# A two-layer streaming-encoder trunk on one core: the rows for the experts' gather are stored with even columns ahead of odd ones, by ScalarE copies, and the experts' transposes read neighbouring columns

## The chip, the cores and the metric

The kernel runs on one core of one Trainium2 chip. The metric is the device time of one execution, in microseconds; lower is better. TensorE (PE) multiplies and transposes, VectorE (DVE) and ScalarE (ACT) work elementwise, GpSimd (POOL) does small work and the gathers, SyncE (SP) issues the loads and stores. Each of these runs its own list of instructions in order; semaphores tie the lists together.

## The reference

Two layers, each on a residual stream `h` of 512 tokens by 1024 columns. Three kinds of attention mix the tokens; the first norm follows, then a router that picks two of 16 experts for every token, then the experts and a gated per-layer embedding, and the second norm.

```python
for i in range(DEPTH):                                  # DEPTH = 2
    ...                                                 # three mixers give mix
    h = layer_norm(DEEPNORM_ALPHA * h + mix, ln1_g[i], ln1_b[i])
    ffn = grouped_moe(h, router_w, router_b, w_gate[i], w_up[i], w_down[i])
    ple = jax.nn.sigmoid(h @ ple_gate[i]) * (p[i] @ ple_proj[i])
    h = layer_norm(DEEPNORM_ALPHA * h + ffn + ple, ln2_g[i], ln2_b[i])

def grouped_moe(h, router_w, router_b, w_gate, w_up, w_down):
    scores = jax.nn.sigmoid((h @ router_w).astype(jnp.float32))
    ...                                                 # best group of four, top 2 in it: gate
    for e in range(N_EXPERTS):                          # 16 experts
        hid = jax.nn.silu(h @ w_gate[e]) * (h @ w_up[e])
        out = out + gate[..., e:e + 1] * (hid @ w_down[e])
    return out
```

## The kernel before, in words

The 512 tokens lie in four tiles of 128 rows, the whole row of 1024 fp32 columns in each (`VB`, `base(t)`). All large products are made of three matmuls each (`mm3`, lines 213 to 215): every operand is split into a high part, cast by ACT, and a low part, the difference, made by VectorE. `split` (L193) does that for activations, `convert` (L201 and L203) for the weights, 1024 columns at a time out of raw buffers (`RAW`, `raw`) that SyncE's loads fill. A raw buffer is loaded again once the subtract of L203 has read it.

In each layer the last part ahead of the experts goes tile by tile, in the order that the string `MLA_REST` names: `n3 n2 n1 t3 l3 n0 t2 l2 t1 l1 t0 l0`.

- `n`: `first_norm(t)` projects the mixers' output, takes the norm (square on ACT at L942, `z` on VectorE at L944, a tile of the pool `w4`, four buffers) and writes the normed row back into `VB` (L951, two halves). Then SyncE stores the row in DRAM (L953, `h1_d`), from where the experts gather it.
- `t`: `rows_to_T` transposes the row in two groups of four (L229, PSUM tags `tr` and `av`) and splits both groups (L193).
- `l`: `logits` multiplies the transposed row by the router's weights (L957, L958).

Behind the last tile stand the router (ACT copies the logits out at L983 as `lgs`; VectorE makes scores, picks and ranks, L984 to L1043; one-hot masks `ohs` at L1050; PE turns them into the table `ti` of token numbers for every expert, L1053 and L1055; the gates end at L1083, and PE's L1060 reads them) and, on PE between all that, the products of the first quarter of the per-layer embedding (`embed`, "mm<-RA" and "s<-RA" 128x256, with ACT's tanh at L922 and VectorE's L923 and L929).

An expert has room for 112 tokens. `fetch_tokens` gathers its rows by an indirect DMA on GpSimd (L1094), which waits for all four stores and for `ti`. `turn_tokens` transposes them eight times (L1126). The gate and up weights are loaded with two neighbouring rows side by side, `"e (j p r) c -> e p j (r c)"` with r=2, so that the contraction index on partition p of piece (j, r) is 256 j + 2 p + r. The transposes therefore read every second column of the gathered row:

```python
def pair_columns(k):
    return slice(256 * (k // 2) + k % 2, 256 * (k // 2 + 1), 2)
```

Then 48 matmuls for gate and up and 24 for down follow, with the hidden rows transposed by four at L1252, and the rows are added into DRAM by an indirect DMA. Expert 0's weights are converted early: the first gate chunk and the up chunk (`raw`) stand among the last tiles' work on ACT and VectorE.

A list scheduler decides when the program is built in which order each engine's instructions stand, by its own estimates; a change of one piece can shift others on every engine. `after(x, [y])` in the code only asks it to keep x behind y.

Of the kernel before, what the change touches and what calls it, by code (L numbers as in the profile page):

```python
# [24 lines left out]
CAP = 112  # L25
# [61 lines left out]
def tile_kernel(ctx, tc, A, out):  # L87
    nc = tc.nc
    V, SC, PE, G = nc.vector, nc.scalar, nc.tensor, nc.gpsimd
# [35 lines left out]
    ID = CT[:, C_ID:C_ID + 128]  # L125
# [6 lines left out]
    h1_d = [dr.tile([S, D], F32, name=f"h1_{i}") for i in range(L)]  # L132
# [4 lines left out]
    def acc(tag="mm"):  # L137
        return ps.tile([128, 512], F32, tag=tag, name=tag)
# [4 lines left out]
    def after(later, earlier, wait=mybir.DependencyClass.NoSync):  # L143

        for e in earlier:
            tc.add_manual_dep(later.ins, e.ins.name, mybir.DependencyInfo(wait, mybir.DependencyReason.DATA),
                              reason="order")
# [19 lines left out]
    tsl = lambda t: slice(t * 128, (t + 1) * 128)  # L167
# [55 lines left out]
    def rows_to_T(row, t, tags=("tr", "tr"), behind=()):  # L223

        subs, his = [], []
        for g in range(2):
            p = acc(tags[g]).rearrange("p (j n) -> p j n", j=4)
            for j in range(4):
                after(PE.transpose(p[:, j], row[:, tsl(4 * g + j)], ID), behind)  # L229
            hi, lo = [R(HS[2 * i + g], 0, 2048, 4)[:, :, tsl(t)] for i in range(2)]  # L230
            done = split(p, hi, lo)
            subs.append(done[1])
            his.append(done[0])
        return subs, his

    def base(t, a=0, b=1024):
        return VB[:, t * 1024 + a:t * 1024 + b]
# [198 lines left out]
    for l in range(L):  # L436
# [407 lines left out]
        for c in ORDER:  # L844
# [10 lines left out]
            elif c == "E":  # L855
# [3 lines left out]
                for i in range(2):  # L859
                    half, t = todo.pop(0)  # L860
# [23 lines left out]
        for kd in range(2):  # L884
            p = trp()
# [48 lines left out]
        def first_norm(t):  # L934
            row = base(t)
            sums = sm.tile([128, 3], F32, name="sums")
            for half in range(2):
                project_o(WO[half], half, t, LATE, 1.0, sums[:, half:half + 1])
            nm = sm.tile([128, 1], F32, name="nm")
            V.tensor_scalar(nm, sums[:, 0:1], sums[:, 1:2], -1.0 / 1024, op0=OP.add, op1=OP.mult)  # L940
            sq = RAW[:, 2, :1024]
            squares[t] = SC.activation(sq, row, AF.Square, bias=nm, accum_out=sums[:, 2:3])  # L942
            z = w4.tile([128, 1024], F32, name="z", tag="w4")
            V.scalar_tensor_tensor(z, row, nm, LN[:, :1024], op0=OP.add, op1=OP.mult)  # L944
            ve = sm.tile([128, 1], F32, name="ve")
            V.tensor_scalar(ve, sums[:, 2:3], 1.0 / 1024, EPS, op0=OP.mult, op1=OP.add)
            rs = sm.tile([128, 1], F32, name="rs")
            pows[t] = G.tensor_tensor(rs, ve, HALF[:, 0:1], op=OP.pow)
            for i in range(2):
                c = slice(512 * i, 512 * i + 512)  # L950
                V.scalar_tensor_tensor(row[:, c], z[:, c], rs, LN[:, 1024 + c.start:1024 + c.stop],  # L951
                                       op0=OP.mult, op1=OP.add)
            nc.sync.dma_start(h1_d[l][tsl(t), :], row)  # L953

        def logits(t):
            for k in range(8):
                PE.matmul(plg[:, t, :32], hT(0, k)[:, tsl(t)], RW[:, k], start=k == 0, stop=False)  # L957
                PE.matmul(plg[:, t, :16], hT(1, k)[:, tsl(t)], RW[:, k, :16], start=False, stop=k == 7)  # L958

        plg = None  # L960
        for c in MLA_REST.split():
            t = int(c[1])
            if c[0] == "a":
                attend_mla(t)
            elif c[0] == "n":
                first_norm(t)
            elif c[0] == "t":
                subs, his = rows_to_T(base(t), t, tags=("tr", "av"))
            elif c[0] == "l":
                if plg is None:  # L970
                    plg = acc("av").rearrange("p (t e) -> p t e", t=4)
                logits(t)
# [133 lines left out]

        def pair_columns(k):
            return slice(256 * (k // 2) + k % 2, 256 * (k // 2 + 1), 2)  # L1110

        def fetch_tokens(e):
            if e == 0:
                xg = raw_chunk([], 1024)[:CAP]
# [6 lines left out]
        def turn_tokens(e, xg):  # L1121
            xh, xl = [R(8 + e % 2, o, 8 * CAP, 8) for o in (0, 1024)]
            for g in range(2):
                p = trp()
                for jj in range(4):
                    PE.transpose(p[:, jj, :CAP], xg[:, pair_columns(4 * g + jj)], ID[:CAP, :CAP])  # L1126
                split(p[:, :, :CAP], xh[:, 4 * g:4 * g + 4], xl[:, 4 * g:4 * g + 4])
            return xh, xl

# [31 lines left out]
        def overflow():  # L1161

            most = nc.values_load(cmi[0:1, 0:1], min_val=0, max_val=S)
            with tc.If(most > CAP, label=f"over{l}"):
                for j in range(1, 5):
                    to, _, *slots_ = slot_tables(j, "o")
                    go = slot_gates(*slots_, "o")
                    nc.sync.dma_start(ov_d[l][0, j - 1].rearrange("e s -> s e"), to)
                    nc.sync.dma_start(ov_d[l][1, j - 1].rearrange("e s -> s e"), go.bitcast(I32))
                i = state["ring"][0]  # L1170
                W = (RAW[:, i] if i < NRAW else state[f"raw{i}"]).rearrange("p (k c) -> p k c", k=4)
                W2 = W.rearrange("p k c -> p (k c)").rearrange("p (k c) -> p k c", k=2)
                with tc.For_i(0, NE, 1) as e:
                    for j in range(4):
                        idx = []
                        for i in range(2):
                            ix = sm.tile([128, 1], I32, name=f"ix{i}")
                            nc.sync.dma_start(ix, ov_d[l][i, j, bass.ds(e, 1), :].rearrange("e s -> s e"))
                            idx.append(ix)
                        xg = w4.tile([128, 1024], F32, name="xg", tag="w4")  # L1180
                        G.memset(xg, 0.0)
                        gather(xg, idx[0])
                        xt = w4.tile([128, 8, 128], F32, name="xt", tag="w4")
                        for g in range(2):
                            p = trp()
                            for jj in range(4):
                                PE.transpose(p[:, jj], xg[:, pair_columns(4 * g + jj)], ID)
                            SC.copy(xt[:, 4 * g:4 * g + 4], p)
                        pgu = []
                        for w in (wgt, wup):  # L1190
                            p = acc("s")
                            for i in range(2):
                                nc.sync.dma_start(
                                    W2, w[bass.ds(e, 1), :, 2 * i:2 * i + 2].rearrange("e p j c -> (e p) j c"))
                                for k in range(4):
                                    PE.matmul(p, xt[:, 4 * i + k], W[:, k], start=i + k == 0, stop=i + k == 4)
                            pgu.append(p)
                        sg = w2.tile([128, 512], F32, name="sg", tag="w2")
                        SC.activation(sg, pgu[0], AF.Silu)
                        V.tensor_tensor(sg, sg, pgu[1], op=OP.mult)  # L1200
                        p = trp()
                        for kd in range(4):
                            PE.transpose(p[:, kd], sg[:, tsl(kd)], ID)
                        ht = w2.tile([128, 4, 128], F32, name="ht", tag="w2")
                        SC.copy(ht, p)
                        yt = w4.tile([128, 1024], F32, name="yt", tag="w4")
                        py = [acc("s") for _ in range(2)]
                        for i in range(2):
                            nc.sync.dma_start(W2, wdn[bass.ds(e, 1), :, 2 * i:2 * i + 2].rearrange("e p k c -> (e p) k c"))
                            for half in range(2):  # L1210
                                for k in range(2):
                                    PE.matmul(py[half], ht[:, 2 * i + k], W2[:, k, half * 512:half * 512 + 512],
                                              start=i + k == 0, stop=i + k == 2)
                        for half in range(2):
                            V.tensor_scalar(yt[:, half * 512:half * 512 + 512], py[half], idx[1].bitcast(F32), None,
                                            op0=OP.mult)
                        scatter(yt, idx[0], y_d[l])
# [11 lines left out]
        xg = fetch_tokens(0)  # L1229
# [8 lines left out]
        for e in range(NE):  # L1238
# [38 lines left out]
            if e + 1 == NE:  # L1277
# [25 lines left out]
                for half in range(2):  # L1303
                    c = slice(512 * half, 512 * half + 512)
# [146 lines left out]
```

## Time and profile before

| | |
|---|---|
| time, median of 3 runs | 1342.89 us (1337.99 to 1343.95) |
| profiled execution | 1344.58 us, its span 1342.8 us, mean granted PE clock 0.976 |
| PE busy | 1284.1 us (96%), 6828 instructions |
| VectorE busy | 1002.9 us (75%) |
| ScalarE busy | 833.8 us (62%) |
| GpSimd busy | 229.3 us (17%) |
| layer 0: last tiles and router | about 262 to 326 us |
| layer 0: experts | about 326 to 665 us |
| layer 1: last tiles and router | about 930 to 985 us |
| layer 1: experts | about 985 to 1320 us |

The busy shares are averages over stages with different limits, so the windows by stage and the timelines of single stretches are read beside them. In a timeline, a row gives the start, the duration, the engine, the line, the operation with its tiles, and in brackets the idle time of the engine ahead of it with what ended it. Matmuls are pipelined, so the distance from one start to the next says more than a duration. Lines in rows are those of the kernel before; the change moves the later ones by 8 or 9 (L958 becomes L966, L983 L992, L1050 L1059, L1055 L1064) and those from `turn_tokens` on by 6 (L1126 becomes L1132).

### The profile page before, as it was taken

The numbers are of one execution on the slowest core, as the hardware profiler recorded it, in microseconds if no ns is written. First come the engines' busy times: TensorE is split into PE (matmuls) and PEld (weight loads), VectorE is DVE, ScalarE is ACT, GpSimd is POOL, SyncE is SP. The second block draws the span as 40 slices with busy tenths as digits, with TensorE's granted clock in tenths as the row PEclk, the third lists the DMA queues.
The fourth block names the chain that finished last, engine by engine and source line by source line (L and its number), as shares of the span: only waits on it lengthen the run. The fifth ranks groups of instructions, "written<-read, shape, count | busy, mean of one in ns | idle before, by whom it ended". The sixth has DMA issues, their size and how long they took to land. (4 is left out here: it accounts for less than half of the span.)

```text
span 1342.8 us, 19139 instructions
## 1 busy us (share of the span) xinstructions
PE 1284.1 (96%) x6828; PEld 1012.9 (75%) x6828; DVE 1002.9 (75%) x1754; ACT 833.8 (62%) x1348; POOL 229.3 (17%) x209
## 2 busy tenths in 40 slices
PE   7899999998999999999889999999989999999996
PEld 6677776777787887777777777767878878778774
DVE  5645768677879879987775557676779797888985
ACT  4544645443868768886444556354467685886873
POOL 2301210001212212222001021200012121221311
PEclk9999998998999999999989999889989999999999
DMA  7732533234989979999763222341469898997983
GB/s 210 263 96 57 194 107 110 94 115 174 331 300 357 368 269 365 368 339 315 269 203 79 64 75 80 87 150 51 164 225 366 289 359 313 337 365 287 381 300 133
DMA packets 126215, 302.36 MB, mean 225 GB/s; under 512 B 13245, under 2 KB 56013, under 8 KB 126112
## 3 DMA queue, kind: packets, MB, share of 16 engines
q1 hardware_dynamic: 115400, 278.29, 57.8%
q0 software_dynamic: 9840, 21.15, 6.5%
q10 hardware_dynamic: 872, 1.62, 0.4%
q8 instruction: 55, 0.90, 0.3%
q14 instruction: 48, 0.39, 0.1%
HBM read 284.92 MB, written 30.39 MB: 235 GB/s over the span
## 5 line engine op out<-in xcount | busy, mean ns | idle before, releaser
L201 ACT CAST RA<-RAW 128x1024 fp32r<-128x1024 f32 x252 | 257.3, 1050 | 67.2 <-PE mm L215 22.9
L203 DVE TENSOR_TENSOR RA<-RAW,RA 128x1024 fp32r<-128x1024 f32 x190 | 227.5, 1222 | 59.3 <-ACT RA L201 56.3
L201 ACT CAST RA<-raw 128x1024 fp32r<-128x1024 f32 x190 | 195.7, 1048 | 61.6 <-PE mm L215 31.5
L203 DVE TENSOR_TENSOR RA<-raw,RA 128x1024 fp32r<-128x1024 f32 x142 | 168.9, 1220 | 21.2 <-ACT RA L201 20.8
L213 PE MATMUL mm<-RA,slot 128*112 128x512 f32 (+2 forms) x424 | 175.6, 415 | 4.3 <-ACT RAW L740 3.2
L215 PE MATMUL mm<-RA 128*128 128x512 f32 (+1 forms) x400 | 153.5, 384 | 0.7 <-DVE RA L193 0.7
L215 PE MATMUL mm<-RA,slot 128*112 128x512 f32 (+2 forms) x360 | 146.5, 407 | 0.0
L1099 POOL DMA_INDIRECT y<-yt,ti x30 | 64.6, 2152 | 476.0 <-ACT yt L1275 476.0
L214 PE MATMUL mm<-RA,slot 128*112 128x512 f32 (+2 forms) x344 | 141.3, 411 | 0.9 <-DVE RA L203 0.9
L213 PE MATMUL mm<-RA 128*128 128x512 f32 (+1 forms) x336 | 127.8, 381 | 5.9 <-ACT RA L201 3.7
L214 PE MATMUL mm<-RA 128*128 128x512 f32 (+1 forms) x336 | 126.7, 377 | 2.1 <-DVE RA L203 2.1
L213 PE MATMUL av<-RA 128*112 128x512 f32 x256 | 103.4, 404 | 0.8 <-ACT RA L201 0.8
L215 PE MATMUL av<-RA 128*112 128x512 f32 x256 | 101.8, 397 | 0.7 <-DVE RA L193 0.6
L213 PEld LDWEIGHTS mm<-RA,slot 128*112 128x112 f32 (+1 forms) x424 | 79.6, 188 | 26.5 <-ACT RAW L740 4.2
L213 PE MATMUL s<-RA,ht 128*112 128x512 f32 x240 | 94.9, 395 | 0.4 <-ACT ht L193 0.4
L215 PE MATMUL s<-RA,ht 128*112 128x512 f32 x240 | 94.6, 394 | 0.0
L215 PEld LDWEIGHTS mm<-RA 128*128 128x128 f32 x400 | 77.5, 194 | 12.6 <-issue 2.4
L215 PEld LDWEIGHTS mm<-RA,slot 128*112 128x112 f32 (+1 forms) x360 | 66.7, 185 | 19.7 <-issue 0.9
L214 PEld LDWEIGHTS mm<-RA,slot 128*112 128x112 f32 (+1 forms) x344 | 65.3, 190 | 18.1 <-issue 1.7
L203 DVE TENSOR_TENSOR slot<-RAW,RA 128x1024 fp32r<-128x1024 f32 x62 | 73.7, 1220 | 6.5 <-ACT RA L201 6.5
L213 PEld LDWEIGHTS mm<-RA 128*128 128x128 f32 x336 | 65.4, 195 | 15.3 <-ACT RA L201 4.1
L213 PE MATMUL s<-RA 128*128 128x256 f32 (+3 forms) x256 | 75.6, 296 | 0.5 <-ACT RA L193 0.3
(425 smaller groups left out, 2888.6 us busy)
## 6 DMA issues: line engine op xcount, KB each, us to landing
RAW<-in_w_gate_dram SPq DMA_DIRECT2D x56, 1024.0 KB
raw<-in_w_down_dram SPq DMA_DIRECT2D x45, 1024.0 KB
raw<-in_w_up_dram SPq DMA_DIRECT2D x40, 1024.0 KB
RAW<-in_w_up_dram SPq DMA_DIRECT2D x24, 1024.0 KB
RAW<-in_w_down_dram SPq DMA_DIRECT2D x19, 1024.0 KB
RAW<-in_w_in_dram SPq DMA_DIRECT2D x26, 512.0 KB
RAW<-in_w_o_dram SPq DMA_DIRECT2D x16, 512.0 KB
raw<-in_w_gate_dram SPq DMA_DIRECT2D x8, 1024.0 KB
```

The lines of the kernel that those rows point to most:

```text
L201: cast = SC.copy(hi[:, a:b], raw[:, a:b])
L203: state["subs"] = [V.tensor_sub(lo[:, a:b], raw[:, a:b], f32(hi[:, a:b]))]
L213: PE.matmul(o, sh, mh, start=start, stop=False)
L214: PE.matmul(o, sh, ml, start=False, stop=False)
L215: return PE.matmul(o, sl, mh, start=False, stop=stop)
L1099: G.indirect_dma_start(out=dst, out_offset=bass.IndirectOffsetOnAxis(ap=idx.bitcast(U32), axis=0), in_=src, in_offset=None, bounds_check=S ...
```

## The change

The store of a normed row moves from `first_norm` to a new function `store_rows`, which runs behind `rows_to_T` of the same tile. It copies the row from `VB` into `z` with two ACT copies of 128x512; in every block of 256 columns the 128 even ones come first and the 128 odd ones behind. The copies are asked to stand behind both casts of the tile. SyncE then stores `z`. The transposes of the gathered rows take neighbouring columns (`tsl`), since what was column 256 j + 2 p + r is now column 256 j + 128 r + p. `VB` itself keeps its order. (The last edit is in the path for experts with over 112 tokens, which these inputs do not take.)

```diff
-            nc.sync.dma_start(h1_d[l][tsl(t), :], row)
+            return z
+
+        def store_rows(t, z, behind):
+
+            for i in range(2):
+                c = slice(512 * i, 512 * i + 512)
+                after(SC.copy(z[:, c].rearrange("p (j r i) -> p j r i", j=2, r=2),
+                              base(t)[:, c].rearrange("p (j i r) -> p j r i", j=2, r=2)), behind)
+            nc.sync.dma_start(h1_d[l][tsl(t), :], z)
...
-        plg = None
+        plg, normed = None, {}
...
-                first_norm(t)
+                normed[t] = first_norm(t)
             elif c[0] == "t":
                 subs, his = rows_to_T(base(t), t, tags=("tr", "av"))
+                store_rows(t, normed[t], his)
...
-        def pair_columns(k):
-            return slice(256 * (k // 2) + k % 2, 256 * (k // 2 + 1), 2)
-
...
-                    PE.transpose(p[:, jj, :CAP], xg[:, pair_columns(4 * g + jj)], ID[:CAP, :CAP])
+                    PE.transpose(p[:, jj, :CAP], xg[:, tsl(4 * g + jj)], ID[:CAP, :CAP])
...
-                                PE.transpose(p[:, jj], xg[:, pair_columns(4 * g + jj)], ID)
+                                PE.transpose(p[:, jj], xg[:, tsl(4 * g + jj)], ID)
```

With this the scheduler's order comes out differently in the stretch ahead of the experts. Below stands the order of the instructions, by line, operation and tiles, without times.

ScalarE, layer 0, from the cast of the projection weights to the logits' copy and what follows it, before. L193 casts are those of `split` (`tr` and `av` are the two halves of a tile's transposes, `pj` the embedding's projection weights), L201 casts those of weights, L911 scales a finished row:

```order
L193 CAST pj<-pr__4185 128x512
L201 CAST RA<-RAW 128x1024 x2
L193 CAST RA<-av 128x4x128
L193 CAST RA<-tr 128x4x128
L911 ACTIVATE VB<-VB 128x256 x2
L193 CAST RA<-av 128x4x128
L201 CAST RA<-RAW 128x1024 x2
L983 COPY lgs<-av 128x128
L911 ACTIVATE VB<-VB 128x256
L985 ACTIVATE sco<-sco 128x64
```

The same place in the changed kernel:

```order
L193 CAST pj<-pr__4193 128x512
L201 CAST RA<-RAW 128x1024
L193 CAST RA<-av 128x4x128
L959 COPY z<-VB 128x512 x2
L193 CAST RA<-tr 128x4x128
L201 CAST RA<-RAW 128x1024
L911 ACTIVATE VB<-VB 128x256 x2
L193 CAST RA<-av 128x4x128
L959 COPY z<-VB 128x512 x2
L201 CAST RA<-RAW 128x1024
L992 COPY lgs<-av 128x128
L201 CAST RA<-RAW 128x1024
```

The copies of tiles 1 and 0 (L959) stand in between (tile 2's stand just ahead, tile 3's further up), and one of the two weight casts that stood right ahead of `lgs` now stands behind it.

VectorE, layer 0, in the router's chain from the ranks' operand `B` to the token table `ti`, before:

```order
L1038 TENSOR_TENSOR B<-oh,CT 128x8x16
L1042 TENSOR_TENSOR tmp<-oh,av 128x128
L1089 TENSOR_REDUCE cmx<-av 128x1
L1043 TENSOR_REDUCE rank<-tmp 128x8
L1091 CAST cmi<-cmx 128x1
L1050 TENSOR_SCALAR ohs<-IOB,rank 128x128 x8
L1070 TENSOR_TENSOR tmp<-oh,sco 128x128
L923 SCALAR_TENSOR_TENSOR th<-th,s 128x256
L1055 TENSOR_SCALAR ti<-av 128x16
```

And before, further down on the same engine, behind the last of the gates (`B<-oh,gb`), the two subtracts of the raw up-weights (`RA<-raw`):

```order
L929 SCALAR_TENSOR_TENSOR VB<-VB,th 128x256
L1083 TENSOR_TENSOR B<-oh,gb 128x8x16
L203 TENSOR_TENSOR RA<-raw_4308,RA 128x1024
L1064 TENSOR_TENSOR gs<-vv 128x16
L203 TENSOR_TENSOR RA<-raw_4308,RA 128x1024
L1065 TENSOR_TENSOR gs<-gs,vv 128x16
```

The chain from `B` to `ti` in the changed kernel:

```order
L1047 TENSOR_TENSOR B<-oh,CT 128x8x16
L203 TENSOR_TENSOR RA<-raw_4316,RA 128x1024
L1051 TENSOR_TENSOR tmp<-oh,av 128x128
L1098 TENSOR_REDUCE cmx<-av 128x1
L1052 TENSOR_REDUCE rank<-tmp 128x8
L1100 CAST cmi<-cmx 128x1
L203 TENSOR_TENSOR RA<-raw_4316,RA 128x1024
L1059 TENSOR_SCALAR ohs<-IOB,rank 128x128 x8
L1079 TENSOR_TENSOR tmp<-oh,sco 128x128
L923 SCALAR_TENSOR_TENSOR th<-th,s 128x256
L1064 TENSOR_SCALAR ti<-av 128x16
```

Both subtracts of `raw` now stand inside the chain: one ahead of `tmp`, one ahead of the masks `ohs`. In layer 1 only one of them does, the one ahead of `ohs`.

On TensorE nine more of embed's 128x256 matmuls stand ahead of the second group of transposes of the last tile, so ahead of the last logits; the matmuls that turn `ohs` into `ti`, which alternated with embed's last ones, stand behind all of these; and those that make the ranks stand 11 places further back. On SyncE the load of expert 0's remaining up-weights, which waits for the second subtract, still follows the four stores and the loads it followed before.

## Rows read from the trace of the kernel before

**Rows 1.** The page: busy time by engine; GB/s in 40 slices of the span.

```profile
PE 1284.1 (96%) x6828; PEld 1012.9 (75%) x6828; DVE 1002.9 (75%) x1754; ACT 833.8 (62%) x1348; POOL 229.3 (17%) x209
...
GB/s 210 263 96 57 194 107 110 94 115 174 331 300 357 368 269 365 368 339 315 269 203 79 64 75 80 87 150 51 164 225 366 289 359 313 337 365 287 381 300 133
```

**Rows 2.** Windows: PE, PEld, DVE, ACT, POOL busy; PE clock; DMA share; GB/s.

```profile
302.00:326.00 24.00, 19.33 (x182) 18.68 (x180) 20.13 (x78) 9.37 (x18) 1.40 (x2) 0.94 0.37 130
...
500.00:600.00 100.00, 100.00 (x465) 76.74 (x464) 89.78 (x92) 84.61 (x101) 24.02 (x15) 1.00 0.98 354
```

**Rows 3.** Waits of PE, 326 to 665 us: total, times, longest (first row).

```profile
PE av L213 <- ACT RA L201: 0.8, 1, 0.8
```

**Rows 4.** Groups by line and shape, weight loads: busy, mean ns | idle before.

```profile
L1126 PEld LDWEIGHTS trp<-CT,xg 112*128 112x128 f32 x240 | 33.4, 211 | 2.9
...
L1252 PEld LDWEIGHTS trp<-CT,sg 112*128 112x128 f32 x128 | 15.0, 140 | 5.7 <-DVE sg L1243 1.2
```

**Rows 5.** Timeline of PE: two transpose groups and the matmul behind each.

```profile
334.07 1.09 PE L1126 MATMUL trp<-CT,xg 112*128 112x112 f32 x8
334.93 0.46 PE L215 MATMUL mm<-RA,slot 128*112 128x512 f32 x1
...
343.82 0.55 PE L1252 MATMUL trp<-CT,sg 112*128 112x112 f32 x4
344.14 0.46 PE L213 MATMUL av<-RA 128*112 128x512 f32 x1
```

**Rows 6.** Timeline of PE: the first expert's transposes, layer 0.

```profile
324.51 1.74 PE L1126 MATMUL trp<-CT,RAW 112*128 112x112 f32 x8 [1.38 <-DMA RAW<-h,ti]
...
326.12 0.77 PE L213 MATMUL mm<-RA,slot 128*112 128x512 f32 x1
```

**Rows 7.** Timeline of ACT: a cast that waits for its load.

```profile
637.71 2.00 ACT L201 CAST RA<-RAW 128x1024 fp32r<-128x1024 f32 x2 [1.74 <-DMA RAW<-in_w_up_dram]
```

**Rows 8.** Timeline of ACT: last tiles of layer 0 up to the logits' copy.

```profile
295.86 0.59 ACT L193 CAST RA<-tr 128x512 fp32r<-128x512 f32 x1 [5.97 <-PE tr L229]
...
298.43 0.64 ACT L193 CAST pj<-pr__4185 128x512 fp32r<-128x512 f32 x1
298.95 2.01 ACT L201 CAST RA<-RAW 128x1024 fp32r<-128x1024 f32 x2
...
305.13 0.59 ACT L193 CAST RA<-av 128x512 fp32r<-128x512 f32 x1 [2.31 <-PE av L229]
...
308.00 0.27 ACT L983 COPY lgs<-av 128x128 f32<-128x128 f32 x1 [0.39 <-PE av L958]
```

**Rows 9.** Timeline of PE: the first and the eleventh of a run of embed matmuls.

```profile
310.04 0.28 PE L214 MATMUL s<-RA 128*128 128x256 f32 x1
...
311.23 0.28 PE L215 MATMUL s<-RA 128*128 128x256 f32 x1
```

**Rows 10.** Timeline of DVE: the router's chain in layer 0, and behind it.

```profile
309.89 0.19 DVE L986 TENSOR_SCALAR sco<-sco 128x64 f32<-128x64 f32 x1
...
314.94 0.28 DVE L1038 TENSOR_TENSOR B<-oh,CT 128x128 bf16<-128x128 f32 x1
315.72 0.29 DVE L1042 TENSOR_TENSOR tmp<-oh,av 128x128 f32<-128x128 f32 x1 [0.50 <-PE av L1035]
...
316.37 1.40 DVE L1050 TENSOR_SCALAR ohs<-IOB,rank 128x128 bf16<-128x128 bf16 x8
...
318.82 0.17 DVE L1055 TENSOR_SCALAR ti<-av 128x16 int32<-128x16 f32 x1 [0.53 <-PE av L1053]
...
322.63 1.22 DVE L203 TENSOR_TENSOR RA<-raw,RA 128x1024 fp32r<-128x1024 f32 x1
```

**Rows 11.** Timeline of ACT: the two casts ahead of those subtracts.

```profile
316.18 1.05 ACT L201 CAST RA<-raw 128x1024 fp32r<-128x1024 f32 x1 [7.04 <-PE mm L215]
...
318.50 1.05 ACT L201 CAST RA<-raw 128x1024 fp32r<-128x1024 f32 x1 [0.44 <-PE mm L215]
```

**Rows 12.** Timeline of POOL: the first expert's gather, layer 0.

```profile
319.88 1.12 POOL L1094 DMA_INDIRECT RAW<-h,ti  x1 [20.90 <-DVE den L1075]
```

## The prediction

> **What bounds the kernel now.** I read the page's first section, then the windows by stage, then who waits for whom in the longest stage, and last the timelines of the two places that the diff touches. The page's first line shows TensorE busy for 1284.1 of 1342.8 us, VectorE for 1002.9 [rows 1]. The windows say where that share is not full: from 500 to 600 us, with the first layer's experts running, PE is busy for the whole 100 us, while between 302 and 326 us, where that layer's router runs, it has 19.33 of 24 us [rows 2]. So there are two kinds of place. In the expert stage every nanosecond taken from PE comes off the time: the largest wait of PE's in the first layer's is a single one of 0.8 us [rows 3]. In the router's stretch of each layer the time is a chain: last tile's logits, VectorE's scores and ranks, the token table, the gather, the first expert's transposes. A delay of that chain counts in full, because PE has nothing else left.
>
> **What the transposes give.** The 240 LDWEIGHTS of `turn_tokens` that read every second column of a gathered row take 211 ns, the 128 of L1252, of the same 112x128 shape from neighbouring columns, 140 ns [rows 4]. These lie beside matmuls, so I do not count their busy time but the distance between starts. A group of eight transposes starts at 334.07 and the matmul behind it at 334.93: 0.86 us. A group of four from neighbouring columns starts at 343.82 and the next matmul at 344.14: 0.32, so 0.64 for eight [rows 5]. That is 0.22 us for an expert, and 240/8 = 30 experts make 6.6 us. The first expert of each layer is left: its eight start at 324.51, and the next matmul at 326.12, 1.61 us for eight, on an engine that had just waited [rows 6]. Between nothing and the same quarter of 1.61 us (0.4) I take 0.2 for each, 0.4 together.
>
> Not all of it stays. Late in layer 0 the ACT casts of weights wait for their loads, 1.74 us at 637.71 [rows 7], and PE's wait of 0.8 us is one for such a cast [rows 3]. What the last four experts of that layer would give, 4 x 0.22 = 0.9 us, I take as lost to the loads. Bounds: nothing lost, or all 3.3 us of the layer. The transposes give 6.6 + 0.4 - 0.9 = **6.1 us** (bounds 3.7 and 7.0).
>
> **What the copies cost.** Sixteen ACT copies of 128x512 are new, eight for a layer. No row shows a copy with a stride of two. The nearest are the ACT cast of pj, 128x512, 0.64 us and 0.52 us to the next start, and twice that, 1.05 us, the time of a 128x1024 cast, for the other end [rows 8, 11]. I take 0.52, the row of the same shape; a tile's pair is then 1.05 us. In layer 0 the pair of tile 3 falls into an idle stretch of 5.97 us. The pairs of tiles 2 and 1 push the later casts by 2.1 us, and the idle time of 2.31 us ahead of the last cast takes these 2.1 in [rows 8]. The pair of tile 0 stands ahead of `lgs`, but of the two weight casts that stood between (such a pair takes 2.01 us) one has moved behind `lgs`. ACT is therefore ready at about 308.7, and is not what `lgs` waits for.
>
> What it waits for is PE, where nine more embed matmuls stand ahead of the last tile's second transposes. They run 0.12 us apart (ten from 310.04 to 311.23) [rows 9], so `lgs` moves from 308.00 to 309.05: **+1.05**. The cast that moved behind `lgs` and its subtract (1.05 + 1.22 us) then hold up L986, which stands behind that subtract on VectorE: about 311.5 instead of 309.89, +1.6 [rows 10].
>
> Now the largest term. Both subtracts of the raw chunk (expert 0's first up-weights), of which the first ran at 322.63, behind everything the router needs, 1.22 us each, stand in the middle of the router's chain in the changed order: one ahead of L1042, one ahead of the eight `ohs` of L1050 [rows 10]. Each waits for an ACT cast, and the casts wait for the embed matmuls that last read the same slots: 316.18 after 7.04 us of idleness, 318.50 after 0.44 [rows 11]. With `B` of L1038 at 316.55 (314.94 + 1.6) and the first cast done by 316.9, the first subtract ends at 317.9, and L1042 starts there, where it was at 315.72: +2.2. The second cast waits for the last embed matmul, which comes earlier than before, since the `ohs` matmuls no longer stand between: 317.65 to 318.7. Its subtract ends at 319.85, and `ohs` starts at 319.9 instead of 316.37: +3.5. From `ohs` to `ti` it took 2.45 us, 0.53 of it a wait for matmuls that alternated with embed's; alone on PE they follow the masks at once, so 1.85, and `ti` moves from 318.82 to 321.75, **+2.9** [rows 10]. The gather at 319.88 [rows 12] and the transposes at 324.51 [rows 6] follow it by the same 2.9.
>
> Layer 1 repeats the pattern, but only one subtract stands in the chain there: the same steps give +2.3. The front costs 2.9 + 2.3 = **5.2 us**. Lower bound: `lgs` late by 1.05 and the subtracts' 2.44 or 1.22, less the 0.50 + 0.53 us that the chain waits now [rows 10], so 2.5 + 1.2 = 3.7. A gain is excluded, because work is added to a chain that has less idle time than that. Upper bound: copies at 1.05 each, which take 2.1 us for a tile; then ACT has 4.2 us to hide in 2.31 and ends tile 0's pair and the one cast at 310.6, 1.5 later than PE's 309.05: 8.2 for both layers.
>
> The other edits cost nothing that ends a chain. The last store leaves behind tile 0's pair, at about 307.7, and the gather is 12 us further on [rows 12]. The buffers `z` are held until their stores land; the cast of pj, which takes one over from tile 3, stands 8 us behind that store. L911 no longer waits for the stores. SyncE issues the next up-weights sooner, since the second subtract frees their buffer sooner, and the first expert, which waits for its tokens, doesn't run sooner for it.
>
> **The sum.** The profiled execution took 1344.58 us, 1.8 more than its span and 1.7 more than the median of 1342.89. 1344.58 - 6.1 + 5.2 = 1343.7; taken from the median it is **1342.0**. The working range is 1339.6 (7.0 gained, 3.7 lost) to 1345.0 (8.2 lost).
>
> **Rivals.** *The loads become the bound; slower.* An expert is six chunks of 128x2048 fp32, 6.3 MB, which takes 17.8 us at the 354 GB/s that the window from 500 to 600 us moves while PE is never idle. PE quicker by 0.22 us asks for 1.2% more, 358 GB/s. If the transfers can't do that, PE's gain turns into waits for weights, and only the front's cost is left: 1342.9 + 5.2 = 1348.1, more with dear copies (1351.1). For it: the DMA share of 0.98 in that window [rows 2], and the late waits [rows 7]. Against it: one slice of the page shows 381 GB/s [rows 1], and 6.3 MB at that take 16.5 us. It decides from the point where the transfers stay under 358 GB/s.
>
> *The whole difference of the weight loads shows; faster.* 240 x 71 ns [rows 4] = 17.0 us, so 1342.9 - 17.0 + 5.2 = 1331.1. It needs LDWEIGHTS to set PE's pace there. Against it are the starts, 107 ns apart with the stride and 80 without [rows 5].
>
> *A stride of two costs nothing.* Then the 140 ns differ from 211 for another reason (four in a group instead of eight, or another tile), the transposes are no quicker, and the time is 1348.1. The rows of starts and of durations both speak against it [rows 4, 5]. [...]
>
> *Copies at 1.05 us,* as above: 1342.9 - 6.1 + 8.2 = 1345.0.
>
> **Chances.** The forecast 0.60, loads bound 0.13, weight loads whole 0.08, stride free 0.07, dear copies 0.08, anything else 0.04. A measurement of this kernel can tell about 0.5% from no change, 6.7 us. Below 1336.2 lies the second rival, and 0.02 of the unnamed: 0.10. Above 1349.6 lies about a third of the two cases at 1348.1, and 0.02 of the unnamed: 0.09. The rest, 0.81, is within. The range runs from 1337.0 (the forecast's 1339.6 less 2.6, since the three runs lie from 1337.99 to 1343.95 and so the median itself may move) to 1348.5 (both cases at 1348.1 in it).
>
> **What would show it.** In the trace of the changed kernel: LDWEIGHTS of the gathered rows at about 140 ns and 0.64 us from a group's start to the next matmul; copies of about 0.6 us; `lgs` about 1 us later, L1059's `ohs` 3.5 us later in layer 0, the first transposes 2.9 and 2.3 us later against each layer's start; PE still without waits over 2 us in the experts. I am wrong if the chain from `lgs` to `ti` is as long as before, if the casts of weights wait for DMA all through the experts, or if starts stay 107 ns apart.

## The result, and the profile of the changed kernel

The changed kernel takes 1350.53 us in the median (1349.76 to 1353.65, six runs) where the kernel before takes 1341.95 (1337.99 to 1345.37, six runs): 8.6 us more, ratio 1.0076 with an interval of 1.0062 to 1.0090 (the two medians alone give 1.0064). The forecast was 1342.0 in a range of 1337.0 to 1348.5, with 0.09 for slower by over 0.5%. It is slower by more than that, and outside the range.

The profiled execution took 1350.95 us with a span of 1349.2, 6.4 more than the span before. The busy time hardly moved; the first line of its page answers to [rows 1]:

```profile
PE 1282.1 (95%) x6828; PEld 1006.9 (75%) x6828; DVE 1002.5 (74%) x1754; ACT 842.0 (62%) x1364; POOL 226.2 (17%) x209
```

PE is busy for 2 us less and ACT for 8 more, so what the time went into is waiting. Where, is read from the starts of the first and the last expert's transposes in each layer. Timeline of PE in the changed kernel, the first and the last group of layer 0, then of layer 1 (a count under x8 is a group that the edge of the window has cut; here only the starts matter):

```profile
328.20 0.61 PE L1132 MATMUL trp<-CT,RAW 112*128 112x112 f32 x2 [1.44 <-DMA RAW<-h,ti]
...
621.47 0.74 PE L1132 MATMUL trp<-CT,xg 112*128 112x112 f32 x6
...
987.46 0.79 PE L1132 MATMUL trp<-CT,RAW 112*128 112x112 f32 x3 [1.16 <-DMA RAW<-h,ti]
...
1299.70 0.83 PE L1132 MATMUL trp<-CT,xg 112*128 112x112 f32 x7
```

And in the kernel before, the last of layer 0 (its first is in [rows 6]), then the first and the last of layer 1:

```profile
619.65 0.62 PE L1126 MATMUL trp<-CT,xg 112*128 112x112 f32 x4
...
984.71 1.74 PE L1126 MATMUL trp<-CT,RAW 112*128 112x112 f32 x8 [1.07 <-ACTq L1164]
...
1293.64 0.73 PE L1126 MATMUL trp<-CT,xg 112*128 112x112 f32 x5
```

From the first to the last, layer 0 took 295.14 us before and 293.27 after, 1.87 less: the transposes' gain, less a loss of about 1 us that is told below. Layer 1 took 308.93 and 312.24, **3.31 more**, where the same gain was expected. The rest is ahead of the first transposes. There I measure from the ACT cast that ends the long idle time (295.86 in [rows 8], 296.54 after), which takes out the 0.68 us by which the two executions differ up to that point. ACT and VectorE of the changed kernel in layer 0, the rows that answer to [rows 8] and [rows 10]:

```profile
296.54 0.59 ACT L193 CAST RA<-tr 128x512 fp32r<-128x512 f32 x1 [4.71 <-PE tr L229]
...
309.77 0.27 ACT L992 COPY lgs<-av 128x128 f32<-128x128 f32 x1 [0.23 <-PE av L966]
```

```profile
312.17 0.19 DVE L995 TENSOR_SCALAR sco<-sco 128x64 f32<-128x64 f32 x1
...
317.50 1.23 DVE L203 TENSOR_TENSOR RA<-raw,RA 128x1024 fp32r<-128x1024 f32 x1
318.64 0.28 DVE L1051 TENSOR_TENSOR tmp<-oh,av 128x128 f32<-128x128 f32 x1
...
319.38 1.22 DVE L203 TENSOR_TENSOR RA<-raw,RA 128x1024 fp32r<-128x1024 f32 x1
320.52 1.38 DVE L1059 TENSOR_SCALAR ohs<-IOB,rank 128x128 bf16<-128x128 bf16 x8
...
322.36 0.16 DVE L1064 TENSOR_SCALAR ti<-av 128x16 int32<-128x16 f32 x1
```

| later than before, less 0.68 us | forecast | measured |
|---|---|---|
| logits' copy `lgs` | 1.05 | 309.77 - 308.00 - 0.68 = 1.09 |
| L995 (L986 before) | 1.6 | 312.17 - 309.89 - 0.68 = 1.60 |
| `tmp`, L1051 (L1042) | 2.2 | 318.64 - 315.72 - 0.68 = 2.24 |
| `ohs`, L1059 (L1050) | 3.5 | 320.52 - 316.37 - 0.68 = 3.47 |
| `ti`, L1064 (L1055) | 2.9 | 322.36 - 318.82 - 0.68 = 2.86 |
| first transposes, layer 0 | 2.9 | 328.20 - 324.51 - 0.68 = 3.01 |

In layer 1 the same cast stands at 957.07 after and 956.34 before, so its first transposes come 2.75 - 0.73 = 2.02 us later (forecast 2.3). Both fronts make 5.0 us. Now 5.0 - 1.9 + 3.3 = 6.4, the difference of the spans; what is left (0.68 more ahead of the first front, 1.09 less between the layers, 0.34 more behind the last transposes) cancels. The fronts are as forecast; the surprise lies within layer 1's experts.

It lies between two experts' transposes there. They start at 1014.72 and 1032.70 before, 17.98 us apart, and at 1018.59 and 1040.54 after, 21.95. (The first of each pair are the third expert's; PE still has the second expert's products to finish behind them.) Timeline of ACT, then of PE, in the changed kernel:

```profile
1020.95 2.00 ACT L201 CAST RA<-RAW 128x1024 fp32r<-128x1024 f32 x2
1027.16 1.99 ACT L201 CAST RA<-RAW 128x1024 fp32r<-128x1024 f32 x2 [4.21 <-PE mm L215]
1029.06 0.52 ACT L193 CAST ht<-trp 128x448 fp32r<-128x448 f32 x1
```

```profile
1027.16 0.40 PE L215 MATMUL mm<-RA,slot 128*112 128x512 f32 x1
1029.64 0.49 PE L213 MATMUL s<-RA,ht 128*112 128x512 f32 x1 [2.08 <-ACT ht L193]
```

ACT stands idle for 4.21 us ahead of a weight cast. Behind that cast in its list stands the cast of `ht`, the hidden rows, for which PE has to wait 2.08 us. The windows show what follows that wait (columns as in [rows 2]):

```profile
1027.10:1029.60 2.50, 0.46 (x2) 0.01 (x1) 1.23 (x1) 2.44 (x4) 0.00 (x0) 1.00 1.05 340
1029.60:1034.00 4.40, 4.36 (x12) 2.94 (x13) 4.03 (x4) 3.02 (x4) 0.00 (x0) 0.62 1.02 387
```

For 4.4 us after the wait the granted clock averages 0.62. From 1031.00 to 1034.00 it is 0.50, and the 128x512 matmuls there start 0.43 us apart, where they started 0.23 us apart at 1026.70, with the clock at 1.00 from 1015 to 1027. Wait and clock together, 2.08 + 4.4 x 0.38 = 3.8 us, make most of the 4.1 (21.95 - 17.98, and the 0.17 that this expert should have been quicker).

What ended ACT's idle time is not the matmul that the row names. The cast's twin in the kernel before waited 0.33 us for the matmul that frees its slot:

```profile
1019.32 1.05 ACT L201 CAST RA<-RAW 128x1024 fp32r<-128x1024 f32 x1 [0.33 <-PE mm L215]
```

The matmul of the same place in the changed kernel is over by 1023, and the cast starts at 1027.16. Layer 0 of the changed kernel has a smaller idle time in its second expert too, and there the row names no releaser at all ("issue" is time in which the engine waited for nothing that the profile shows):

```profile
358.94 1.05 ACT L201 CAST RA<-raw 128x1024 fp32r<-128x1024 f32 x1 [2.24 <-issue]
```

PE waits 0.32 and 1.08 us behind it, and the distance of those two experts' transposes is 19.74 us, where it was 18.79. So the questions for the chip were three: what the transposes give by themselves, what the two subtracts cost, and what stops ACT.

### The profile page after: what moved, and what is told of

Read it like the earlier page. It is cut to its first block, busy times and chain, and to the rows that moved or that the text cites. A ratio compares the mean times of both kernels' runs of the same rounds, so it can differ in the third digit from the quotient of the medians.

```text
span 1349.2 us, 19153 instructions
## 1 busy us (share of the span) xinstructions
PE 1282.1 (95%) x6828; PEld 1006.9 (75%) x6828; DVE 1002.5 (74%) x1754; ACT 842.0 (62%) x1364; POOL 226.2 (17%) x209
## 5 line engine op out<-in xcount | busy, mean ns | idle before, releaser
L201 ACT CAST RA<-RAW 128x1024 fp32r<-128x1024 f32 x252 | 257.4, 1050 | 67.6 <-PE mm L215 28.2
L201 ACT CAST RA<-raw 128x1024 fp32r<-128x1024 f32 x190 | 196.0, 1048 | 62.5 <-PE mm L215 29.6
L1108 POOL DMA_INDIRECT y<-yt,ti x30 | 61.2, 2041 | 481.8 <-ACT yt L1281 481.8
L213 PE MATMUL s<-RA,ht 128*112 128x512 f32 x240 | 95.5, 398 | 2.1 <-ACT ht L193 2.1
L215 PE MATMUL s<-RA,ht 128*112 128x512 f32 x240 | 95.2, 397 | 0.0
L214 PE MATMUL s<-RA,ht 128*112 128x512 f32 x192 | 76.3, 398 | 0.0
## 6 DMA issues: line engine op xcount, KB each, us to landing
RAW<-in_w_gate_dram SPq DMA_DIRECT2D x56, 1024.0 KB, 10.2
RAW<-in_w_up_dram SPq DMA_DIRECT2D x24, 1024.0 KB, 10.2
```

Source lines behind the costliest of these rows:

```text
L201: cast = SC.copy(hi[:, a:b], raw[:, a:b])
L213: PE.matmul(o, sh, mh, start=start, stop=False)
L214: PE.matmul(o, sh, ml, start=False, stop=False)
L215: return PE.matmul(o, sl, mh, start=False, stop=stop)
L1108: G.indirect_dma_start(out=dst, out_offset=bass.IndirectOffsetOnAxis(ap=idx.bitcast(U32), axis=0), in_=src, in_offset=None, bounds_check=S ...
```

## The experiments

**Transposes alone.** In the kernel before, one line:

```diff
-                    PE.transpose(p[:, jj, :CAP], xg[:, pair_columns(4 * g + jj)], ID[:CAP, :CAP])
+                    PE.transpose(p[:, jj, :CAP], xg[:, tsl(4 * g + jj)], ID[:CAP, :CAP])
```

> The kernel before with one line changed: turn_tokens reads neighbouring columns, while the rows are stored in their old order, so expert inputs are permuted columns and the products are not those of the reference. The order of all instructions is that of the kernel before. If the transposes' gain is real and stays (0.17 us for each of 30 experts, from the distance of two experts' transposes in the two traces, 18.01 and 17.84), the time is 5.1 us less: 1336.8, ratio 0.996. If loads eat it, 1341 to 1342.

Measured: 1338.57 us beside 1341.10, 2.5 less; ratio 0.9982 (0.9968 to 0.9995), so 0.7 to 4.3 us. The gain is real, and the 5.1 us that the distance of experts promises lie just outside that interval. The weight loads of the transposes in this kernel (groups by line and shape):

```profile
L1126 PEld LDWEIGHTS trp<-CT,xg 112*128 112x128 f32 x240 | 25.7, 140 | 4.5
```

That is the 140 ns of [rows 4]'s second row, against 211 with the stride. In the trace, experts in the middle of a layer are 17.84 us apart instead of 18.01, but the last of layer 0 is 18.39 instead of 18.05, and the first two of layer 1 are 10.12 apart instead of 8.98. In these two PE's clock comes up: it is 0.50 for the first 4 us in both kernels, and in the rest 0.98 before and 0.79 here. Their distance differs from kernel to kernel, 8.4 to 10.2 us in those shown here. From the first to the last transposes layer 0 takes 1.89 us less than before and layer 1 1.16 less, 3.05 together.

**Copies and order alone.** In the changed kernel the line above is turned back.

> The changed kernel with the strided transposes put back, so the copies and the moved order alone; expert inputs are permuted columns, and the products are not those of the reference. If the two halves add up, the time is that of the changed kernel plus 5.1 us, 1355.6, ratio 1.010, with PE's extra 4 us in layer 1's third expert again. If the late weights in the third expert come from PE being quicker (it asks for weights sooner), that stall is gone here and the time is 1350 to 1352.

Measured: 1353.26 us beside 1341.10, ratio 1.0079 (1.0059 to 1.0100), 12.2 us by the medians. By the medians, each taken from its own kernel before, it is 3.6 us slower than the changed kernel; by the ratios (1.0079 and 1.0076) the two can't be told apart. Its experts are 18.01 us apart again, and the idle time of ACT is there again, at the same cast:

```profile
ACT RA L201 <- PE mm L215: 4.3, 1, 4.3
```

(waits of ACT between 1005 and 1032 us: total, times, longest). So it isn't that a quicker PE asks for its weights too early.

**The copies' stride.** As the last, with plain copies.

```diff
-                after(SC.copy(z[:, c].rearrange("p (j r i) -> p j r i", j=2, r=2),
-                              base(t)[:, c].rearrange("p (j i r) -> p j r i", j=2, r=2)), behind)
+                after(SC.copy(z[:, c], base(t)[:, c]), behind)
```

> The copies and the moved store alone, with plain copies in place of the strided ones, and strided transposes as before: the same work in the same order as c_only but for the copies' stride. What is asked is the price of the stride in a copy: 660 ns for each in the changed kernel. If the stride costs nothing they take 640 to 660 ns here too, as the cast of pj does; if it costs, 500 to 600 ns.

Measured, in one execution of each: 1354.35 us beside 1342.56, with the same idle time (4.1 us). The copies' groups, in the changed kernel and here:

```profile
L959 ACT COPY z<-VB 128x512 f32<-128x512 f32 x16 | 9.8, 660 | 0.0
```

```profile
L959 ACT COPY z<-VB 128x512 f32<-128x512 f32 x16 | 9.1, 621 | 0.0
```

A stride of two costs an ACT copy 39 ns of 660, between the two cases forecast, so 0.6 us of busy time for all sixteen. The price taken in the sum, 0.52 us a copy in a row, was somewhat low: a pair takes 1.21 to 1.24 us in the trace, for 1.05.

**The subtracts behind the masks.** In the changed kernel, one condition: both up chunks of expert 0, not the second alone, have their subtracts behind `ohs`.

```diff
-            elif (w, e, i) == ("u", 0, 1):
+            elif (w, e) == ("u", 0):
                 state["first"] = [ohs_made]
```

> The changed kernel with one condition more: the subtracts of expert 0's first up chunk are asked to stand behind the masks ohs, where they stood before. If the front's cost is the subtracts, ohs comes 2.4 us (layer 0) and 1.5 us (layer 1) sooner than in the changed kernel, and with it the first transposes; if the late weights of layer 1's third expert follow from the late front, their 4 us go too: 1342 to 1343, ratio about 1.000. If those 4 us have another cause, 1346 to 1347.

Measured: 1342.34 us beside 1341.10, ratio 1.0008 (0.9992 to 1.0024). Its VectorE in layer 0:

```profile
317.31 1.39 DVE L1059 TENSOR_SCALAR ohs<-IOB,rank 128x128 bf16<-128x128 bf16 x8
319.15 0.17 DVE L1064 TENSOR_SCALAR ti<-av 128x16 int32<-128x16 f32 x1
322.95 1.22 DVE L203 TENSOR_TENSOR RA<-raw,RA 128x1024 fp32r<-128x1024 f32 x1
```

The subtract is back behind the chain. Measured from the same cast (295.49 here), `ohs` comes 2.2 us sooner than in the changed kernel, and the first transposes are 0.4 us later than before in layer 0 and 0.9 in layer 1, together 1.4 instead of 5.0. So the subtracts cost 3.7 us of the front, the moved matmuls and casts the rest. ACT's idle time in layer 1 has not gone, it has changed:

```profile
1015.73 1.05 ACT L201 CAST RA<-RAW 128x1024 fp32r<-128x1024 f32 x1 [0.18 <-PE mm L215]
1019.54 1.05 ACT L201 CAST RA<-RAW 128x1024 fp32r<-128x1024 f32 x1 [2.76 <-PE mm L215]
```

It is 2.76 us, and one cast further on. PE waits 0.82 us behind it, and the two transposes are 19.09 us apart instead of 21.95, so the time came out as forecast for a stall that has gone. A load that comes late would stop the same cast in every kernel. Something that goes with the place in ACT's list of instructions would not.

**One copy for a tile.** In the changed kernel, without the condition above:

```diff
-            for i in range(2):
-                c = slice(512 * i, 512 * i + 512)
-                after(SC.copy(z[:, c].rearrange("p (j r i) -> p j r i", j=2, r=2),
-                              base(t)[:, c].rearrange("p (j i r) -> p j r i", j=2, r=2)), behind)
+            after(SC.copy(z.rearrange("p (j r i) -> p j r i", j=4, r=2),
+                          base(t).rearrange("p (j i r) -> p j r i", j=4, r=2)), behind)
```

> The changed kernel with the two copies of a tile made one of 128x1024, so four ACT instructions fewer in each layer; the order puts both subtracts back behind the masks. The copies' work on ACT is the same or a little less (no second start). If the subtracts in the router's chain cost the 2 to 3 us of each front, ohs is within 1.2 us of the kernel before. If the 4 us of idle ACT in layer 1 (second expert, the cast that the trace puts down to a PE matmul long done) come from where ACT's instructions lie in its stream, that idle time moves by some instructions, and is shorter or falls where PE doesn't wait: 1339 to 1341. If it comes from the late front or from loads, it follows the front: gone or as small as in subs_late. Time 1339 to 1343, ratio 0.998 to 1.001.

Measured: 1339.76 us beside 1340.53, ratio 0.9995 (0.9978 to 1.0012). The order alone explains the front: the subtracts stand behind the chain again, and the first transposes are 0.2 and 0.6 us later than before. ACT's idle time of layer 1:

```profile
1019.42 0.60 ACT L1244 ACTIVATE sg<-mm 112x512 f32<-112x512 f32 x1 [0.35 <-PE mm L215]
1024.53 2.94 ACT L201 CAST RA<-raw 128x1024 fp32r<-128x1024 f32 x3 [4.50 <-issue]
```

It lasts 4.50 us and stands several instructions further on than in subs_late, with four ACT instructions fewer in each layer. Here the row itself says "issue": ACT waited for nothing that the profile shows. PE waited only 0.3 us behind it, because `ht` was already cast.

**The copies on GpSimd.** In the changed kernel:

```diff
-                after(SC.copy(z[:, c].rearrange("p (j r i) -> p j r i", j=2, r=2),
+                after(G.tensor_copy(z[:, c].rearrange("p (j r i) -> p j r i", j=2, r=2),
```

> The changed kernel with the copies on GpSimd instead of ACT; the order on ACT, VectorE and PE is then nearly that of the kernel before. If the copies' place on ACT (and what it makes of the order) is what costs, this has the gain alone: 1336.8 to 1338, ratio 0.996 to 0.997. If the copies cost wherever they are (GpSimd slow with a stride, VectorE slowed beside it), 1340 to 1345.

Measured: 1338.16 us beside 1341.10, ratio 0.9982 (0.9968 to 0.9996): the gain of the transposes alone, 2.9 us, with the whole computation done. This one is quicker than both kernels. A pair of copies takes 1.7 us there, behind the power of the same tile's norm:

```profile
281.68 0.56 POOL L948 TENSOR_TENSOR rs<-ve,HALF 128x1 f32<-128x1 f32 x1 [9.32 <-DVE ve L946]
282.17 1.70 POOL L959 COPY z<-VB 128x512 f32<-128x512 f32 x2
289.20 0.54 POOL L948 TENSOR_TENSOR rs<-ve,HALF 128x1 f32<-128x1 f32 x1 [5.33 <-DVE ve L946]
```

GpSimd is idle for 5.33 us even after them, so they delay no norm. Layer 1 has none of the long idle time on ACT at that place. Layer 0 has one, in its second expert, with `ht` behind it, and PE waits 1.7 us for that:

```profile
355.93 1.06 ACT L201 CAST RA<-RAW 128x1024 fp32r<-128x1024 f32 x1
361.24 2.94 ACT L201 CAST RA<-RAW 128x1024 fp32r<-128x1024 f32 x3 [4.25 <-issue]
```

**Instructions without work.** To the kernel with GpSimd's copies, tiny ACT copies of 128x1 are added, two for each tile (as many instructions as the changed kernel's copies), and in a second run four:

```diff
+            for i in range(2):
+                spare = sm.tile([128, 1], F32, name="spare", bufs=2)
+                after(SC.copy(spare, CT[:, 0:1]), behind)
             nc.sync.dma_start(h1_d[l][tsl(t), :], z)
```

> The kernel with GpSimd's copies, and beside them two tiny ACT copies of 128x1 for each tile, as many ACT instructions as the changed kernel has copies, with next to no work (about 0.2 us each). If the 4 us of idle ACT in layer 1 hang on the number of ACT instructions ahead of them, they come back here, at about the same cast of the second expert, and PE waits some 2 us there: 1341 to 1343, ratio 1.000 to 1.002. If they hang on the late front, on the loads or on the copies' work, there are none: 1338 to 1339, ratio 0.998.

> As pool_pad2, with four tiny ACT copies for each tile. By the theory of the instructions' place the idle time of ACT comes about 16 instructions earlier in its stream than in pool_pad2, so some 6 to 10 us earlier, and PE waits for another cast or for none: 1338 to 1343. By the others no such idle time: 1338 to 1339.

Measured: with two, 1342.34 us beside 1340.53, ratio 1.0007 (0.9988 to 1.0027); with four, 1341.21, ratio 0.9999 (0.9980 to 1.0019). ACT in layer 1 with two, then with four:

```profile
1017.92 1.05 ACT L201 CAST RA<-RAW 128x1024 fp32r<-128x1024 f32 x1 [0.34 <-PE mm L215]
1021.86 0.53 ACT L193 CAST ht<-trp 128x448 fp32r<-128x448 f32 x1 [2.88 <-PE mm L215]
```

```profile
1008.72 1.99 ACT L201 CAST RA<-raw 128x1024 fp32r<-128x1024 f32 x2
1013.64 1.99 ACT L201 CAST RA<-RAW 128x1024 fp32r<-128x1024 f32 x2 [2.94 <-PE av L215]
```

The idle time that the kernel with GpSimd's copies doesn't have in layer 1 is back with sixteen instructions that do next to nothing, ahead of `ht`, and PE waits 1.40 us for it. With sixteen more it stands eight casts earlier in the list, and PE waits 1.70 us for another cast. It hangs on the number of instructions ahead of it.

The place can be counted in the traces, with every instruction of ACT and of its sequencer. In layer 1 the idle time ends at ACT's 1483rd instruction or at the one behind it in all seven kernels that have it, whatever that instruction is and whenever it comes. In layer 0 all ten kernels have one, of 1.5 to 4.3 us, at the 517th to the 520th. The three without it in layer 1 (the kernel before, the one with the transposes alone, the one with GpSimd's copies) reach the 1483rd 71 instructions behind the jump over the overflow path, the other seven 42 to 62 behind it.

What moves then can be seen in the DMA queues. In the page of every kernel there are two queues of kind "instruction". Of the windows around the idle times, the row of that kind in the changed kernel (1022 to 1028 us), and with one copy for a tile (1020 to 1026):

```profile
q14 instruction: 2, 0.02, 0.6%
```

```profile
q14 instruction: 1, 0.01, 0.3%
```

One or two packets of some 8 KB in each; the page counts 48 of them in the whole execution. No row names the engine of a packet, but the times tie them to ACT's idle time: in all seventeen cases, seven in layer 1 and ten in layer 0, the last 8 KB packet ends 1.1 to 1.4 us before ACT goes on (in the changed kernel's layer 1 at 1025.92, and ACT goes on at 1027.16). In the three kernels without the idle time in layer 1, the last packet ends about 10 us before ACT reaches the same count. That ACT waits for such a packet there is concluded from this, from the "issue" in three of the rows, and from the way the idle time keeps its place in the count; no row shows the wait itself.

In every kernel with the idle time it comes in the first experts behind the jump over the overflow path (L1170), 38 to 62 instructions behind the jump, not at it. There are one or two such places in a kernel, of 1.5 to 4.5 us each.

## Why the prediction was wrong

Two steps failed. The transposes were put at 6.1 us less, from 0.22 us for an expert, and gave 2.5. And the copies were charged for their own work and for the order ahead of the experts, with the rest at nothing ("The other edits cost nothing that ends a chain"; "PE still without waits over 2 us in the experts"); the runs showed ACT idle for 4.21 us in layer 1's second expert, at a fixed place in its list of instructions, a wait of PE's of 2.08 us behind it, and 4.1 us lost. The two make 3.6 + 4.1 = 7.7 of the 8.5 us between the forecast and the median.

*The front* was right, step by step: 1.09, 1.60, 2.24, 3.47, 2.86 and 3.01 us where 1.05, 1.6, 2.2, 3.5, 2.9 and 2.9 were forecast, 5.0 us in the two layers for 5.2. The order of the instructions, with the durations of the trace before, was enough for that. subs_late and after_one confirm the cause: with the subtracts behind the chain, the two fronts cost 1.4 and 0.8 us.

*The transposes* were over-valued. A group of eight and the matmul behind it in the changed kernel:

```profile
1040.54 0.93 PE L1132 MATMUL trp<-CT,xg 112*128 112x112 f32 x8
1041.24 0.47 PE L213 MATMUL mm<-RA,slot 128*112 128x512 f32 x1
```

They are 0.70 us apart, not 0.64: the price of two groups of four did not carry over to one of eight. So 0.16 for an expert, 30 x 0.16 = 4.8. Of these, the runs with the transposes alone kept 2.5 (0.7 to 4.3), where the forecast kept 6.1. Less than half of the sum's gain was there. In the trace with the transposes alone 3.05 us are left of the 30 x 0.17 = 5.1: the last distance of layer 0 lost 0.5 (18.39 instead of 18.05, and the 0.17), where 0.9 had been set aside for the loads, and the first of layer 1 lost 1.3 with its lower clock, in which the kernels differ. The 0.4 us for the first expert of each layer did not show: the eight transposes and the step to the next matmul take 1.61 us in layer 0 in both kernels.

*The missing term* is ACT's idle time in layer 1, 4.1 us, and no rival had it. The rival with the right sign, loads that become the bound, had the wrong mechanism: c_only has slower transposes and the same stall, and in pool_pad2 sixteen empty instructions bring it back with the experts' loads as they were. The copies had been charged by their work on ACT, which was indeed covered. That they also move every later instruction in ACT's list was not charged, and the trace of before held a hint that I didn't read: an idle time of ACT of 2.73 us in layer 0's second expert, ahead of the cast at 363.18, behind which PE waits 0.35 us for `ht`. By the count and the packet it is the same: it ends at the 520th instruction, 1.25 us behind an 8 KB packet.

*The sum again*, from runs: the transposes 2.5 less, the fronts 5.0 more, the stall 4.1 more make +6.6, against 6.4 between the two profiled spans. (The changed kernel's smaller stall in layer 0 belongs in it too: 19.74 - 18.79 + 0.17 = 1.1 more. So terms and spans agree to about 1 us.) The medians differ by 8.6 and the ratio's interval means 8.3 to 12.1. So 2 us or more are not in this account. The profiled execution of before was itself 2.6 us above its median (1344.58 to 1341.95), that of the changed kernel 0.4, which is about as much; which stretch varies from run to run was not followed further.

*The rival of a free stride* failed, as the trace of before had it: 211 against 140 ns is the stride of the weight loads, since t_only changes nothing else. An ACT copy took 660 ns with the stride and 621 without it.

Not settled: why the packet ends about 10 us before ACT is at that count in some kernels and only 1.1 to 1.4 us before ACT goes on in others, and whether another place of the instructions would let the kernel with GpSimd's copies keep the 1.7 us that PE waits in its layer 0. Counts were varied only as shown.

## What to carry to other kernels

When an edit adds instructions to an engine, look at where it moves the others: the 1.2 us subtracts that slid into the router's chain cost more (3.7 us) than all else that moved in the two fronts (1.4). Give new work to an engine that is idle there, GpSimd here, and hold by an explicit condition what must stay behind a critical chain. And when a wait in a row names a producer that was done long ago, add or take away instructions without work: if the idle time moves with their number, it is neither the producer nor the data, and the count of instructions ahead of it shows its place.

## What the runs showed of the hardware that was not expected

- ACT stood idle for 1.5 to 4.5 us in the second expert of a layer with nothing shown in the profile that it still had to wait for, at the same count of its instructions in every kernel that had it (517 to 520 in layer 0, 1483 or 1484 in layer 1), and went on 1.1 to 1.4 us behind an 8 KB packet of an instruction queue. 16 instructions of 128x1 brought such a stall into layer 1 and 16 more moved it eight casts earlier.
- A wait of PE's of 2.08 us was followed by 4.4 us at a granted clock of 0.62, so it cost about twice its length (2.08 + 4.4 x 0.38 = 3.8 us).
- fp32 weight loads from every second column took 211 ns, from neighbouring ones 140, but the transposes came only about 20 ns closer together (0.86 and 0.70 us for eight).
- GpSimd's strided copies of 128x512, 0.85 to 0.89 us each, ran beside VectorE's chain without the kernel becoming slower than with the transposes alone (1338.16 and 1338.57 us).
